# Log-sum-exp over rows: joined bulk loads, a shifted row mix, and the store's wait moved to the end of SyncE's closing waits

## Chip, cores and metric

The kernel runs on one core of one Trainium2 chip. The metric is the device time of one execution in microseconds. "Span" is what the trace of one profiled execution covers from its first to its last instruction; the measured time of the same execution is about 1.8 us longer.

## The reference

```python
def setup_inputs():
    batch, seq, dim = 32, 512, 1024
    return {"x": np.random.randn(batch, seq, dim).astype(np.float32)}

def reference(x):
    max_x = np.max(x, axis=-1, keepdims=True)
    return (max_x.squeeze(-1) + np.log(np.sum(np.exp(x - max_x), axis=-1))).astype(np.float32)
```

There are 16384 rows of 1024 floats: 67.1 MB to read and 64 KB to write. The kernel lays them out as 128 partitions with 128 rows each ("row" below is one row in every partition).

## The kernel before

It takes the exponential without subtracting the maximum, sums, takes the logarithm, and checks at the end that all sums were in a safe range. A slow path, never taken with these inputs, redoes everything with the maximum.

```python
RING = 48                      # rows of buffer in each partition
loads = [
    "R6 R5 R5", "R6 R5 R5", "R8 R8", "R8 R8", "R4 R4 R3 R3 A A", "R6 T3 T3", "R6 A A", "R4 T2",
    "R3 R3", "R3", "A A A", "R2 A", "T2", "T2", "T1", "A", "A",
]
```

Each string is one load and what is done with its rows. ScalarE always computes the exponential. For "R" VectorE reduces the rows, for "T" VectorE adds a row's two halves with an accumulator, for "A" ScalarE accumulates by itself, one instruction for each row.

```python
def load(p0, c0, size, i):
    step = {2: 4, 3: 2, 4: 2}.get(i, 1)      # loads 2, 3, 4 in interleaved pieces
    return [nc.sync.dma_start(out=ring[k::step, p0 : p0 + size, :],
                              in_=source(c0, size)[k::step]).ins for k in range(step)]
# ... cut: the loop over loads
if how == "A":
    exp = nc.scalar.activation(out=o, in_=v, func=AF.Exp, accum_out=sums)
else:
    exp = nc.scalar.activation(out=v, in_=v, func=AF.Exp)
# ... cut
if how == "R":
    added = [nc.vector.reduce_sum(out=sums, in_=v, axis=AX.X)]
elif how == "T":
    ...  # scalar_tensor_tensor(lo, lo, 1.0, hi, mult, add, accum_out=sums of the row)
# ... cut: after row 118, ScalarE's logarithm of the first 112 columns and a first check
nc.scalar.activation(out=res[:, W:NC], in_=sumexp[:, W:NC], func=AF.Ln)
nc.sync.dma_start(out=out_rows, in_=res[:, 0:W])
nc.sync.dma_start(out=out_rest, in_=res[:, W:NC])      # the last store, 8 KB
# ... cut: last check, then a branch that ScalarE and VectorE take from its result
```

All transfers are issued by SyncE. They use eight completion semaphores in turn, numbered 102, 103 and 105 to 110 in the trace. At the end SyncE waits for all eight and for the other engines. These waits stand at and in front of an instruction that the trace calls a drain (six records from 159.94 to 161.09 us, the drain at 161.16), and after it all engines meet in a closing barrier (from 161.16 us on).

## Time and profile before

| | before |
|---|---|
| time | 163.68 us, median of 3 (163.54 to 163.72) |
| span of the profile | 162.0 us |
| HBM read | 67.11 MB at 415 GB/s over the span |
| VectorE, ScalarE busy | 123.2 us, 116.2 us |
| last load complete | 158.11 us |

The page gives busy time by engine and by DMA queue; windows give the same for stretches of time; a waits line says engine, line of the kernel, what ended the wait, then total us, number, longest. The one thing that no view prints is the landing of each transfer; the trace has it as the completions on the transfer's semaphore, 384 for the 24 transfers, so 16 each, and the landing times below are the last of each 16.

### The profile page before, as it was taken

The page shows a single profiled execution, that of the slowest core. Times are in us where ns is not written, and L with a number is a line of the kernel's source. Part 1 is how long each engine was busy: PE and PEld are TensorE (multiplying, and loading weights), DVE is VectorE, ACT ScalarE, POOL GpSimd, SP SyncE. Part 2 cuts the span into 40 slices and gives each one's busy share as a digit, 9 for nine tenths or more (in the row PEclk, how much of TensorE's full clock was granted, in tenths as well). Part 3 has the DMA queues.
Part 4 walks back from the last instruction along what each step waited for, and adds up shares of the span by engine and source line. Part 5 has one row for each costly group of instructions (what it writes and reads, how often), then busy time and mean ns, then how long its engine had stood idle before and what let it go on. Part 6 is the DMA issues. An engine that isn't in the chain of part 4 may idle for free.

```text
span 162.0 us, 224 instructions
## 1 busy us (share of the span) xinstructions
PE 0.6 (0%) x8; PEld 0.3 (0%) x8; DVE 123.2 (76%) x58; ACT 116.2 (72%) x50; POOL 0.2 (0%) x4
## 2 busy tenths in 40 slices
PE   0000000000000000000000000000000000000001
PEld 0000000000000000000000000000000000000000
DVE  0000002999959997299995999999999999999982
ACT  3000069980899609994299914999999998999993
POOL 0000000000000000000000000000000000000000
DMA  7997997998899899799699698899899999999990
GB/s 275 502 518 340 437 518 340 437 518 388 388 518 421 356 518 437 340 518 486 291 518 486 291 518 388 388 449 457 388 429 435 431 395 425 431 419 415 420 359 6
DMA packets 2818, 67.19 MB, mean 415 GB/s; under 512 B 640, under 2 KB 640, under 8 KB 1024
## 3 DMA queue, kind: packets, MB, share of 16 engines
q1 hardware_dynamic: 2816, 67.18, 96.9%
q14 instruction: 2, 0.02, 0.0%
HBM read 67.11 MB, written 0.07 MB: 415 GB/s over the span
## 4 chain that ended last, share of the span: by engine, by line
DMA 52%; DVE 36%; ACT 9%; issue 1%; SPq 0%; PE 0%; DVEq 0%; ACTq 0%
DMA ring<-in_x_dram 52%; DVE sumexp L143 35%; ACT ring L133 9%; DVE ring L148 1%; SPq L88 0%; DVE bad L195 0%; PE count L199 0%; DVE clamped L105 0%; DVE bad L196 0%; DVE fine L201 0%; DVE clamped L109 0%; PE count L200 0%; DVEq L195 0%; DVEq L105 0%; ACTq L133 0%
## 5 line engine op out<-in xcount | busy, mean ns | idle before, releaser
L143 DVE TENSOR_REDUCE sumexp<-ring 128x3 f32<-128x3072 f32 (+5 forms) x21 | 113.9, 5479 | 34.1 <-ACT ring L133 34.0
L133 ACT ACTIVATE ring<-ring 128x3072 f32<-128x3072 f32 (+6 forms) x27 | 104.4, 3921 | 42.5 <-DMA ring<-in_x_dram 42.5
L131 ACT ACTIVATE ring<-ring 128x1024 f32<-128x1024 f32 x9 | 9.4, 1040 | 0.0
L148 DVE SCALAR_TENSOR_TENSOR ring<-ring 128x512 f32<-128x512 f32 x13 | 8.3, 687 | 0.7 <-ACT ring L133 0.7
L75 ACT ACT_TABLE_LOAD x1 | 1.3, 1283 | 0.8 <-PEq L262 0.8
L131 ACT ACTIVATION_READ_ACCUMULATOR ring<-ring 128x1 f32 x9 | 1.7, 186 | 0.0
L148 DVE DVE_READ_ACCUMULATOR ring<-ring 128x1 f32 x13 | 1.1, 84 | 0.0
L131 ACT ACTIVATE last_exp<-ring 128x1024 f32<-128x1024 f32 x1 | 1.0, 1028 | 0.0
L113 PE MATMUL count<-far,bad 128*1 128x1 f32 x4 | 0.4, 164 | 158.5 <-DVE clamped L109 158.5
L76 DVE MEMSET ones<- 128x1 f32 x1 | 0.1, 59 | 0.9 <-PEq L262 0.9
L105 DVE TENSOR_SCALAR clamped<-sumexp 128x118 f32<-128x118 f32 (+1 forms) x2 | 0.4, 198 | 0.2
L195 DVE TENSOR_REDUCE bad<-ring 128x1 f32<-128x64 f32 x1 | 0.2, 220 | 0.4 <-issue 0.4
L109 DVE SCALAR_TENSOR_TENSOR clamped<-clamped,sumexp 128x118 f32<-128x118 f32 (+1 forms) x2 | 0.5, 226 | 0.1
L113 PEld LDWEIGHTS count<-far,bad 128*1 128x1 f32 x4 | 0.2, 80 | 158.6 <-DVE clamped L109 158.6
L201 DVE TENSOR_SCALAR fine<-count 1x1 int32<-1x1 f32 x1 | 0.1, 147 | 0.3 <-PE count L200 0.3
L168 ACT ACTIVATE res<-sumexp 128x112 f32<-128x112 f32 x1 | 0.3, 279 | 0.0
L188 ACT ACTIVATE res<-sumexp 128x16 f32<-128x16 f32 x1 | 0.2, 215 | 0.0
L199 PE MATMUL count<-far,bad 128*1 128x1 f32 x2 | 0.2, 164 | 0.6 <-DVE bad L196 0.6
L200 PE MATMUL count<-ones,sumexp 128*1 128x1 f32 x2 | 0.2, 163 | 0.0
L131 ACT ACTIVATION_READ_ACCUMULATOR last_exp<-ring 128x1 f32 x1 | 0.2, 186 | 0.0
L196 DVE TENSOR_SCALAR bad<-bad 128x1 f32<-128x1 f32 x1 | 0.2, 154 | 0.0
L109 DVE DVE_READ_ACCUMULATOR clamped<-clamped,sumexp 128x1 f32 x2 | 0.2, 84 | 0.0
(7 smaller groups left out, 0.6 us busy)
## 6 DMA issues: line engine op xcount, KB each, us to landing
ring<-in_x_dram SPq DMA_DIRECT2D x1, 6144.0 KB, 28.8
ring<-in_x_dram SPq DMA_DIRECT2D x2, 3072.0 KB, 28.0
ring<-in_x_dram SPq DMA_DIRECT2D x3, 1536.0 KB, 29.5
ring<-in_x_dram SPq DMA_DIRECT2D x1, 4096.0 KB, 27.7
ring<-in_x_dram SPq DMA_DIRECT2D x2, 1024.0 KB, 30.2
ring<-in_x_dram SPq DMA_DIRECT2D x3, 512.0 KB, 26.1
ring<-in_x_dram SPq DMA_DIRECT2D x10, 37.6
out_dram<-res SPq DMA_DIRECT2D x1, 56.0 KB, 8.9
```

The costliest lines, as they stand in the source:

```text
L75: nc.scalar.preload_act_table_set("natural_log_exp_and_others")
L105: nc.vector.tensor_scalar(out=clamped[:, c0:c1], in0=sumexp[:, c0:c1], scalar1=LOW, scalar2=HIGH, op0=ALU.max, op1=ALU.min,)
L109: counted = nc.vector.scalar_tensor_tensor(out=clamped[:, c0:c1], in0=clamped[:, c0:c1], scalar=0.0, in1=sumexp[:, c0:c1], op0=ALU.bypass, ...
L113: nc.tensor.matmul(count, lhsT=bad[:, i : i + 1], rhs=far, start=i == 0, stop=False)
L131: exp = nc.scalar.activation(out=o, in_=v, func=AF.Exp, accum_out=sums)
L133: exp = nc.scalar.activation(out=v, in_=v, func=AF.Exp)
L143: added = [nc.vector.reduce_sum(out=sums, in_=v, axis=AX.X)]
L148: nc.vector.scalar_tensor_tensor(out=lo, in0=lo, scalar=1.0, in1=ring[:, p + r, H:d], op0=ALU.mult, op1=ALU.add, accum_out=sums[:, r : r + 1],
L168: ln = nc.scalar.activation(out=res[:, 0:W], in_=sumexp[:, 0:W], func=AF.Ln)
L188: nc.scalar.activation(out=res[:, W:NC], in_=sumexp[:, W:NC], func=AF.Ln)
L195: nc.vector.reduce_max(out=bad[:, 3:4], in_=last_row[:, 0, 0 : d // 16], axis=AX.X)
L196: nc.vector.tensor_scalar(out=bad[:, 2:3], in0=bad[:, 3:4], scalar1=LOG_LOW, scalar2=None, op0=ALU.is_lt)
```

## The change

The intent: fewer transfers and fewer waits on the way (loads 2, 3 and 4 as one transfer each), less work for VectorE in the second half at some cost to ScalarE, and nothing but the barrier left for SyncE to do once the last store has landed.

```diff
     loads = [
-        "R6 R5 R5", "R6 R5 R5", "R8 R8", "R8 R8", "R4 R4 R3 R3 A A", "R6 T3 T3", "R6 A A", "R4 T2",
-        "R3 R3", "R3", "A A A", "R2 A", "T2", "T2", "T1", "A", "A",
+        "R6 R5 R5", "R6 R5 R5", "R8 R8", "R8 R4 R4", "R4 R4 R3 R3 A A", "R6 T3 A A A", "R6 A A",
+        "R2 A A T2", "R3 R3", "R3", "A A A", "T2 A", "T2", "T2", "T1", "A", "A",
     ]
...
-        dmas = load(p, c, size, i)
+        dma = nc.sync.dma_start(out=ring[:, p : p + size, :], in_=source(c, size)).ins
...
+    def look_at_store_last(program):
+        ... # finds SyncE's drain with its list of waits
+        store = last_store.sync_info.on_update[0].id
+        waits = sorted(drain.sync_info.on_wait, key=lambda wait: wait.id != store)
+        ... # the drain gets this list: the store's wait first
+    nc.at_finalize(look_at_store_last)
...
-    nc.sync.dma_start(out=out_rest, in_=res[:, W:NC])
+    last_store = nc.sync.dma_start(out=out_rest, in_=res[:, W:NC]).ins
```

The first wait of the list stays with the drain, and the others become waits in front of it; so "first in the list" is "last in time".

More of the change, by code (lines that the diff above doesn't have):

```diff
@@ L81, in source @@
         return x_rest[:, c0 - W : c0 - W + size, :] if c0 >= W else x_rows[:, c0 : c0 + size, :]
-    def load(p0, c0, size, i):
-        step = {2: 4, 3: 2, 4: 2}.get(i, 1)
-        return [
-            nc.sync.dma_start(
-                out=ring[k::step, p0 : p0 + size, :], in_=source(c0, size)[k::step]
-            ).ins
-            for k in range(step)
-        ]
     def without_wait(ins, group, reason):
@@ L122 @@
             p = 0
-        dmas = load(p, c, size, i)
+        dma = nc.sync.dma_start(out=ring[:, p : p + size, :], in_=source(c, size)).ins
         if i == 0:
-            first_load = dmas[0]
+            first_load = dma
         for how, s in ops:
@@ L153 @@
             for add in added:
-                for dma in dmas:
-                    tc.declare_no_dep(add.ins, dma, reason="ScalarE has waited for it")
+                tc.declare_no_dep(add.ins, dma, reason="ScalarE has waited for it")
                 without_wait(add, "loads", "they came before this one")
@@ L164 @@
             last_row = v
-        for dma in dmas:
-            tc.add_to_no_dep_group("loads", dma)
+        tc.add_to_no_dep_group("loads", dma)
         if c == LATE:
@@ L184, in start_early @@
         top.insert(k, first)
+    def look_at_store_last(program):
+        block, k, drain = next(
+            (b, k, i) for b in program.main_func.blocks for k, i in enumerate(b.instructions)
+            if i.engine == mybir.EngineType.SP and isinstance(i, mybir.InstDrain)
+            and i.sync_info and len(i.sync_info.on_wait) > 2
+        )
+        store = last_store.sync_info.on_update[0].id
+        waits = sorted(drain.sync_info.on_wait, key=lambda wait: wait.id != store)
+        assert waits[0].id == store and len(waits) == len(drain.sync_info.on_wait)
+        sync = mybir.SyncInfo(on_wait=waits, on_update=list(drain.sync_info.on_update))
+        block.instructions[k] = drain.__replace__(sync_info=sync)
     nc.at_finalize(start_early)
+    nc.at_finalize(look_at_store_last)
     nc.scalar.activation(out=res[:, W:NC], in_=sumexp[:, W:NC], func=AF.Ln)
     nc.sync.dma_start(out=out_rows, in_=res[:, 0:W])
-    nc.sync.dma_start(out=out_rest, in_=res[:, W:NC])
+    last_store = nc.sync.dma_start(out=out_rest, in_=res[:, W:NC]).ins
     check(LATE, LAST, 1)
```

## The prediction

> **What bounds the kernel now.** I read the page's head and queues first, then the stages, then the waits of ScalarE, VectorE and SyncE, and last the timeline of the end, because the three parts of the change touch the transfers, the row mix and the end.
>
> ```profile
> span 162.0 us, 224 instructions
> PE 0.6 (0%) x8; PEld 0.3 (0%) x8; DVE 123.2 (76%) x58; ACT 116.2 (72%) x50; POOL 0.2 (0%) x4
> q1 hardware_dynamic: 2816, 67.18, 96.9%
> HBM read 67.11 MB, written 0.07 MB: 415 GB/s over the span
> ```
>
> The 16 DMA engines are busy for 96.9% of the span with 67.11 MB that have to be read whatever the kernel does; VectorE and ScalarE idle for a quarter of it. The stages (start:end, length, then busy time of each engine, clock, DMA share, GB/s) show where the last 3% are:
>
> ```profile
> 0.00:21.80 21.80, 0.00 (x0) 0.00 (x0) 0.09 (x2) 1.28 (x1) 0.20 (x4) 1.00 1.03 433
> 21.80:60.50 38.70, 0.00 (x0) 0.00 (x0) 31.35 (x6) 28.08 (x6) 0.00 (x0) 1.00 1.00 434
> 60.50:99.20 38.70, 0.00 (x0) 0.00 (x0) 32.86 (x5) 27.90 (x4) 0.00 (x0) 1.00 0.99 427
> 99.20:138.10 38.90, 0.00 (x0) 0.00 (x0) 38.84 (x20) 37.74 (x19) 0.00 (x0) 1.00 0.98 421
> 138.10:158.20 20.10, 0.19 (x2) 0.09 (x2) 19.23 (x22) 19.88 (x19) 0.00 (x0) 1.00 0.97 402
> 158.20:162.00 3.80, 0.43 (x6) 0.22 (x6) 0.87 (x6) 1.29 (x3) 0.00 (x0) 1.00 0.04 6
> ```
>
> The DMA share stays at 0.97 or above until 158.2 us (a packet is counted where it starts, hence 1.03). Between 99.2 and 158.2 us both compute engines are as full as the DMA, so this is where they could become the bound; the last 3.8 us belong to no transfer of input. Packet by packet, the first 64 KB packet starts at 1.02 us, the last input packet ends at 157.63 us, and the last row's landing is complete at 158.11 us; in between hardly any time has fewer than 15 packets in flight. So the time is: 158.1 us of streaming, 3.85 us of closing, and 1.7 us that the measured time (163.68 us) has over the span.
>
> The waits say who follows whom:
>
> ```profile
> ACT ring L133 <- DMA ring<-in_x_dram: 42.5, 7, 19.7
> DVE sumexp L143 <- ACT ring L133: 34.0, 4, 26.2
> SPq L88 <- DVE sumexp L143: 98.4, 10, 22.7
> ```
>
> ScalarE waits for loads, VectorE for ScalarE, and SyncE for slots that VectorE frees. The last looks like a bound but is none: each load is issued long before the queue is empty. The load issued at 44.53 us follows one that lands at 60.46; 63.86 follows 79.81; 84.94 follows 99.16; 95.67 follows 113.69; 104.26 follows 123.41; the last at 138.05 follows 156.83. The smallest lead is 14.2 us.
>
> The end, from the timeline:
>
> ```profile
> 156.24 0.69 DVE L148 SCALAR_TENSOR_TENSOR ring<-ring 128x512 f32<-128x512 f32 x1 [0.69 <-ACT ring L133]
> 157.06 1.04 ACT L131 ACTIVATE ring<-ring 128x1024 f32<-128x1024 f32 x1
> 158.13 1.03 ACT L131 ACTIVATE last_exp<-ring 128x1024 f32<-128x1024 f32 x1
> 159.31 0.21 ACT L188 ACTIVATE res<-sumexp 128x16 f32<-128x16 f32 x1
> 159.55 0.34 SPq L190 DMA_DIRECT2D out_dram<-res  x1
> 159.81 0.15 DVE L201 TENSOR_SCALAR fine<-count 1x1 int32<-1x1 f32 x1 [0.33 <-PE count L200]
> ```
>
> The last row's exponential starts 0.02 us after its landing, so neither engine is late there; the store's issue follows it at 159.55 us and lands at 161.08.
>
> [...] 433 to 434 GB/s in the first stages, before packets get small. [...] the unsplit second load lands 19.33 us after the first (41.11 after 21.78), the split ones 19.35 us after their predecessors (60.46, 79.81, 99.16). [...] 1040 ns for 1024 elements, 7020 for 8192, and rows of "A" start 1.04 us apart, so the accumulator read of 186 ns is hidden in the overlap. [...] SyncE's record on the store's semaphore begins at 161.094, 0.014 us after the landing.
>
> **The change part by part.**
>
> *Bulk loads as one transfer.* Loads 2, 3 and 4, of 8.39 MB each, were 4 + 2 + 2 transfers; they become 3. Bytes, packet size (64 KB, one per partition) and number of data packets stay. Removed are five issues of SyncE (0.33 to 0.62 us each, all of them behind a full queue, so worth nothing) and five completion markers on each DMA engine: 3 x (19.35 - 19.33) = 0.06 us of streaming. ScalarE also stops waiting for two to four semaphores before these loads: it starts 0.11 us after landing (60.57 against 60.46) where an unsplit load takes 0.02 (41.13 against 41.11). That is off the path, as ScalarE waits over 5 us for each of these loads.
>
> *Row mix.* From the groups by form, VectorE: R rows (reduce) cost about 1.09 us each (9.87 us for nine, in the timeline from 141.61 us), T rows 0.615 us (start to start), A rows nothing. Three T become A: -1.84; two R become A: -2.2; two R become T: -0.95; one R8 becomes two R4: about 2 x 4.41 - 8.68 = +0.14. Some 4.9 us less for VectorE. ScalarE: three A for one T3 is 3 x 1.04 - (2.75 - 0.09) = +0.46; R2 and two A for R4 is (1.90 - 0.09) + 2.08 - (3.61 - 0.09) = +0.37; R2 to T2 is the same exponential; R8 to two R4 is +0.1 and lies in front of a wait of 5.4 us. So +0.83 us where it matters, between 99.24 and 138.06 us. There ScalarE waits 1.11 us in one place, for the load that lands at 138.03. The 0.83 us fit in, and 0.28 us is left. From 138.06 on the order of ScalarE's work is unchanged. VectorE's gain goes into waiting for ScalarE: at 156.24 us it is already idle for 0.69 us before the last T rows. Neither engine's part moves the last landing or the start of the last exponential. Worth 0.00 us.
>
> *The last wait.* SyncE ends with a row of two-semaphore waits, some 60 ns each when satisfied, then two drains into the closing barrier. In this kernel's program the first wait in an instruction's list stays with the instruction, and the others go in front of it; the store is in the last pair in front of the drain. Put first in the list, it is waited for in the drain itself, and what stands between (161.094 to 161.161) is no longer behind the landing: 0.067 us earlier on SyncE, whose barrier entry moves from 161.223 to about 161.156. But the barrier waits for all engines, and ScalarE enters it at 161.257 (a drain of 97 ns that begins at 161.160, 0.37 us after its last branch); GpSimd goes on at 161.289. So ScalarE is the last by 0.03 us, and SyncE's 0.067 us give almost nothing unless ScalarE's comes earlier. I count 0.02.
>
> Sum: -0.06 + 0.00 - 0.02 = -0.08 us: 163.68 becomes 163.60 us.
>
> **The rivals.**
>
> *ScalarE becomes the bound.* For it: 19.88 of 20.10 us busy from 138.1 to 158.2, and it gets ten more instructions. If my 0.83 us were 1.3, it would start the load of 138.03 late by 0.2 us; but it catches up, for later it waits 0.22 us at 154.29 and the rows until then have slack of some tenths. If it doesn't catch up, the lateness goes one to one to the end: 163.8 to 164.1 us. Against: the activations are all measured, and the sum has little room.
>
> *The last landing moves earlier because slots come free earlier.* For it: SyncE's 98.4 us of waiting for VectorE. Against: the lead of 14 us or more; the queue is never empty. If I misread and it does, at most the streaming's loss against 433.6 GB/s (67.11 MB take 154.8 us, against 156.6 from the first packet to the last) could come back, 1.8 us: 161.9 us. But that loss is the slow first packets (3.1 instead of 2.42 us, some 0.7 us) and the small packets of the tail, and both stay.
>
> *Small stalls move.* VectorE's reduction before the finiteness check begins 0.42 us after the instruction before it with no wait that the trace shows, ScalarE's drain is 0.37 us late likewise, and near 142 us all packets of 12 KB are slow for a while (0.25 us in one load's landing). Instruction counts shift by -2 on VectorE and +10 on ScalarE, so such stalls may move: 0.1 to 0.4 us either way on the closing chain. If ScalarE's drain came earlier, the full 0.067 us of the wait would count.
>
> *The split loads did something good* that their joining loses, such as keeping the queue's start quick. Against: loads 0 and 1 are unsplit, and stream at 434 GB/s.
>
> **Range and chances.** The kernel's own runs lie within 0.18 us. Estimated effects are 0.1 us or less, the stalls up to 0.4: 163.25 to 163.95 us should hold it 8 times in 10. Two per cent is 3.3 us; to gain it the kernel would have to finish before its bytes are in, and to lose it ScalarE would need over four times the added 0.83 us. Faster 0.01, within 2% 0.98, slower 0.01.
>
> **What would show it.** In the changed profile: 2736 packets on q1 (five transfers fewer, 16 completions each) and 67.18 MB; VectorE near 118.2 us busy in 56 instructions, ScalarE near 118.1 in 60; VectorE's wait for ScalarE about 5 us longer in total; ScalarE starting the three bulk loads 0.02 instead of 0.08 to 0.11 us after landing; no empty queue; the last exponential near 158.1; the closing chain still about 3.85 us. I am wrong if ScalarE begins the last row visibly after its landing, if the DMA share falls below 0.97 before the last row, or if the span after the last landing shrinks by much more than 0.07 us.

The 0.09 us between two activations in a row can be read in the trace: three of 2.749 us each took 8.07 us together from 138.06 us, 0.09 us of overlap at each of the two seams.

## The result

| | before | changed |
|---|---|---|
| time, median (range), 6 runs each | 163.67 us (163.54 to 163.74) | 163.64 us (163.55 to 163.91) |
| ratio, 95% interval | | 1.0002 (0.9989 to 1.0015) |
| span of the profile | 161.96 us | 161.76 us |
| last load complete | 158.11 us | 157.95 us |
| last store, issue to landing | 1.53 us | 1.59 us |
| landing to SyncE's drain | 0.08 us | 0.02 us |

A ratio is the mean time of one kernel's runs over that of the other's runs of the same rounds, so not quite the ratio of the medians. The time has not changed.

The page's head of the changed kernel:

```profile
span 161.8 us, 221 instructions
PE 0.8 (0%) x8; PEld 0.3 (0%) x8; DVE 118.5 (73%) x56; ACT 117.2 (72%) x60; POOL 0.2 (0%) x4
q1 hardware_dynamic: 2736, 67.18, 97.0%
```

There are 80 packets fewer for the same bytes. VectorE lost 4.7 us of work and ScalarE gained 1.0. The windows of the second half:

```profile
99.20:138.10 38.90, 0.00 (x0) 0.00 (x0) 36.55 (x15) 38.59 (x28) 0.00 (x0) 1.00 0.98 422
138.10:158.20 20.10, 0.19 (x2) 0.09 (x2) 16.90 (x26) 20.07 (x19) 0.00 (x0) 1.00 0.96 399
158.20:162.00 3.80, 0.57 (x6) 0.26 (x6) 0.69 (x6) 1.14 (x3) 0.00 (x0) 1.00 0.04 6
```

VectorE, 38.84 of 38.90 us busy before in the first of these, is at 36.55; ScalarE fills the second stretch all but completely. The DMA share and the GB/s are those of before to 0.01 and 3 GB/s. ScalarE's start on the load that lands at 138 us, before and changed:

```profile
138.06 8.07 ACT L133 ACTIVATE ring<-ring 128x3072 f32<-128x3072 f32 x3 [1.11 <-DMA ring<-in_x_dram]
138.08 8.07 ACT L122 ACTIVATE ring<-ring 128x3072 f32<-128x3072 f32 x3 [0.28 <-DMA ring<-in_x_dram]
```

Its longer work has taken 0.83 us of the wait there, and it still starts on time. Where VectorE's time went, in the waits:

```profile
ACT ring L122 <- DMA ring<-in_x_dram: 41.3, 6, 19.7
DVE sumexp L132 <- ACT ring L122: 37.2, 6, 26.2
DVE ring L137 <- ACT ring L122: 2.1, 2, 1.5
```

VectorE waits 39.3 us for ScalarE instead of 34.7. The end, from the timeline:

```profile
157.98 1.03 ACT L120 ACTIVATE last_exp<-ring 128x1024 f32<-128x1024 f32 x1
159.16 0.22 ACT L190 ACTIVATE res<-sumexp 128x16 f32<-128x16 f32 x1
159.40 0.34 SPq L192 DMA_DIRECT2D out_dram<-res  x1
159.40 0.14 DVE L203 TENSOR_SCALAR fine<-count 1x1 int32<-1x1 f32 x1 [0.59 <-PE count L202]
```

The last exponential still starts 0.02 us after the last landing, and everything else of the end hangs on it as before. The check's result comes 0.41 us earlier, but nothing waits for it alone.

### The profile page after: what moved, and what is told of

Read it like the earlier page. It is cut to its first block, busy times and chain, and to the rows that moved or that the text cites. A ratio compares the mean times of both kernels' runs of the same rounds, so it can differ in the third digit from the quotient of the medians.

```text
span 161.8 us, 221 instructions
## 1 busy us (share of the span) xinstructions
PE 0.8 (0%) x8; PEld 0.3 (0%) x8; DVE 118.5 (73%) x56; ACT 117.2 (72%) x60; POOL 0.2 (0%) x4
## 4 chain that ended last, share of the span: by engine, by line
DMA 53%; DVE 35%; ACT 10%; issue 1%; PE 0%
DMA ring<-in_x_dram 53%; DVE sumexp L132 35%; ACT ring L122 9%; ACT ring L120 1%; ACT last_exp L120 0%; PE count L202 0%; DVE fine L203 0%
## 5 line engine op out<-in xcount | busy, mean ns | idle before, releaser
L132 DVE TENSOR_REDUCE sumexp<-ring 128x3 f32<-128x3072 f32 (+5 forms) x21 | 109.5, 5276 | 37.2 <-ACT ring L122 37.2
L122 ACT ACTIVATE ring<-ring 128x3072 f32<-128x3072 f32 (+6 forms) x27 | 100.3, 3763 | 41.4 <-DMA ring<-in_x_dram 41.3
L120 ACT ACTIVATE ring<-ring 128x1024 f32<-128x1024 f32 x14 | 14.6, 1040 | 0.0
L137 DVE SCALAR_TENSOR_TENSOR ring<-ring 128x512 f32<-128x512 f32 x12 | 7.7, 687 | 2.1 <-ACT ring L122 2.1
L120 ACT ACTIVATION_READ_ACCUMULATOR ring<-ring 128x1 f32 x14 | 2.6, 187 | 0.0
```

The lines of the kernel that those rows point to most:

```text
L137: nc.vector.scalar_tensor_tensor(out=lo, in0=lo, scalar=1.0, in1=ring[:, p + r, H:d], op0=ALU.mult, op1=ALU.add, accum_out=sums[:, r : r + 1],
```

## The experiments

Twelve kernels ran, each profiled once and timed in up to five rounds beside the kernel before. The table has what the traces show at the end; the texts follow.

| run | time us, median | ratio (95%) | last load complete | store, issue to landing | landing to SyncE's drain |
|---|---|---|---|---|---|
| before again | 163.75 | 0.9998 (0.9986, 1.0010) | 158.24 | 1.58 | 0.09 |
| wait only | 163.67 | 0.9998 (0.9986, 1.0010) | 158.15 | 1.54 | 0.02 |
| loads only | 163.96 | 1.0014 (1.0003, 1.0026) | 158.07 | 1.53 | 0.39 |
| row mix only | 164.11 | 1.0023 (1.0010, 1.0036) | 158.22 | 1.81 | 0.09 |
| changed, store's wait first | 164.06 | 1.0024 (1.0009, 1.0038) | 157.94 | 1.64 | 0.39 |
| changed, eight pieces | 270.05 | 1.6495 (1.6472, 1.6518) | 264.08 | 1.79 | 0.02 |
| changed, light engines | 163.55 | 0.9986 (0.9971, 1.0000) | 158.43 | 1.43 | 0.02 |
| changed, more A | 165.06 | 1.0079 (1.0065, 1.0094) | 158.43 | 1.42 | 0.02 |
| before, two rows to VectorE | 165.10 | 1.0087 (1.0073, 1.0101) | 157.91 | 1.93 | 0.09 |
| changed, two rows to VectorE | 163.60 | 0.9994 (0.9980, 1.0007) | 157.95 | 1.64 | 0.02 |
| changed, both padded | 164.32 | 1.0034 (1.0020, 1.0048) | 158.88 | 1.42 | 0.02 |
| changed, VectorE padded | 164.07 | 1.0020 (1.0006, 1.0034) | 158.72 | 1.43 | 0.02 |

### Before again

No edit.

> The kernel before, unchanged, against itself. It measures what two identical programs differ by, and whether three oddities of the first profile belong to the program or to that one execution: VectorE's 0.42 us without a wait before its last reduction, ScalarE's closing drain that starts 0.37 us after its last branch, and the slow packets near 142 us. If they belong to the program, the new profile has all three at the same places. If they belong to the execution, some are gone or elsewhere and the span is shorter by up to 0.3 us, with no change of the kernel. Timed: ratio 1.000, with an interval of about 0.001.

The ratio is 0.9998. Two of the three oddities belong to the program: VectorE's last reduction again comes late with no wait, and ScalarE's closing drain again begins 0.36 us after its last branch. The slow packets near 142 us are not there (that load lands 3.69 us after the one before it, not 3.91), so they do not belong to the program. The first load landed at 22.11 us instead of 21.78, though: a single trace's landing times are good to some 0.3 us, and only the steps between landings, where nothing disturbs them, are good to 0.02.

### Each part alone

Wait only: the kernel before with the function and the `last_store` of the diff.

> The kernel before with the store's wait moved into SyncE's drain and nothing else. Prediction's theory: SyncE's first drain starts right at the store's landing instead of 0.08 us after it, the waits between are done before; of the 0.067 us between 0.00 and 0.07 reach the end, by whether ScalarE's drain is late. Timed 163.60 to 163.68, not to be told from zero. Rival, that the wait was a real cost: 0.3 us or more off the time.

Loads only:

```diff
-        step = {2: 4, 3: 2, 4: 2}.get(i, 1)
+        step = 1
```

> The kernel before with each of loads 2, 3 and 4 as one transfer and nothing else. The prediction said that five markers fewer give 0.06 us of streaming: bulk loads landing 19.33 us apart. The profile of the changed kernel contradicts it (19.35 us apart, as split); then here too 19.35, and the last landing moves only by what varies from execution to execution (0.2 us). ScalarE starts the bulk loads 0.02 us after landing in both cases. Rival, that splitting helped the queue: 0.3 us or more slower. Timed: within 0.1 us of before.

Row mix only: the two lines of `loads` of the diff.

> The kernel before with the changed row mix and nothing else. Theory: VectorE 118.4 us busy, ScalarE 117.2, VectorE idle 4 us more before its instructions, ScalarE's wait for the load that lands at 138.0 us shrinks from 1.11 to about 0.28 us, the last exponential still starts within 0.05 us of the last landing; time within 0.1 us of before. Rival, that ScalarE's longer work reaches the end: 0.2 us or more slower. Rival, that slots freed earlier speed up the stream: 0.3 us or more faster and a last landing before 157.7 us.

The wait alone did what was expected: the drain starts 0.02 us after the landing, and the time is the same. In that trace ScalarE enters the barrier at 161.29 and SyncE at 161.22 us, so the gain is swallowed there.

The loads alone are slower by 0.2 to 0.3 us, which the theory didn't have, and the rival only for another reason. It isn't the stream: the bulk loads land 19.35 us apart, as in pieces. It is SyncE's end. SyncE's wait for the store after its last issue, in the kernel before, in the loads alone and in the changed kernel:

```profile
SPq L273 <- DMA out_dram<-res: 0.2, 1, 0.2
```

```profile
SPq L273 <- DMA out_dram<-res: 1.2, 1, 1.2
```

```profile
SPq L275 <- DMA out_dram<-res: 0.4, 1, 0.4
```

A longer wait here means that SyncE came to the store's semaphore earlier and had its other waits still to do when the store landed. The trace says why. With 24 transfers the store uses semaphore 110, which is in the last of the closing waits. With 19 it uses 105, which is in the first. So in the loads alone SyncE waits for 105 until 161.07 us and then goes through five more waits, 0.06 us each, and reaches its drain at 161.44, 0.39 us after the landing. The transfer count had moved the store's wait to the worst place, and the third part of the change moves it away again. Parts one and three belong together.

The row mix alone is 0.4 us slower, and the engines are not the reason. ScalarE's last exponential starts 0.03 us after the last landing, and its wait for the load that lands at 138 us did shrink as expected. Two other steps are longer in its trace: one load lands 3.84 us after the one before where 3.69 is usual, and the store takes 1.81 us to land instead of 1.53 and 1.58 in the two traces of the kernel before. This is taken up with the padded kernels below.

### The store's wait in the first place

```diff
+        waits = waits[1:7] + waits[:1] + waits[7:]     # after the sort: the first wait in time
```

> The changed kernel with the store's wait put in the first of SyncE's closing waits, so that all the others come after the landing. It enlarges the disputed cost: five more waits of about 0.06 us behind the landing. Theory: SyncE enters the closing barrier 0.30 to 0.36 us later after the store's landing than in the changed kernel, and as SyncE is last there, the time is 0.3 us longer: 163.95 us. Rival, that the other engines hold the barrier and SyncE's order is of no account: 163.64 us.

It was 164.06 us; the drain begins 0.39 us after the landing against 0.02, and all other landings are those of the changed kernel to 0.03 us.

```profile
SPq L276 <- DMA out_dram<-res: 1.3, 1, 1.3
```

The theory holds, and the order of SyncE's waits costs up to 0.4 us in this kernel. The trace shows SyncE's waits in the same order here as in the loads alone, so this run also stands for the changed kernel without its third part.

### Eight pieces for each bulk load

```diff
-        dma = nc.sync.dma_start(out=ring[:, p : p + size, :], in_=source(c, size)).ins
+        step = 8 if i < 5 else 1
+        dmas = [nc.sync.dma_start(out=ring[k::step, p : p + size, :],
+                                  in_=source(c, size)[k::step]).ins for k in range(step)]
```

> The changed kernel with each of the five bulk loads as eight transfers of every eighth partition: 35 transfers more. It enlarges the prediction's 0.012 us for each transfer saved. If that were right, 35 x 0.012 = 0.42 us more: 164.06 us, bulk loads landing 19.43 us apart. If markers cost nothing while the engines are saturated, as the two profiles together suggest: 19.35 us apart and 163.64 us. Rival, that more issues delay the stream's start: the first load lands later than 21.8 us.

It took 270 us, and failed as a test of the markers, because something far larger came in. A window in the bulk loads of the changed kernel, the same window here, and one after the bulk loads, where loads are whole again:

```profile
22.00:60.00 38.00, 0.00 (x0) 0.00 (x0) 30.83 (x6) 27.90 (x6) 0.00 (x0) 1.00 1.00 435
22.00:60.00 38.00, 0.00 (x0) 0.00 (x0) 11.06 (x2) 14.04 (x3) 0.00 (x0) 1.00 0.96 198
222.00:262.00 40.00, 0.19 (x2) 0.09 (x2) 33.48 (x28) 39.46 (x34) 0.00 (x0) 1.00 1.00 424
```

The DMA engines are busy for 0.96 of the window but move less than half as much: most 64 KB packets take 5.10 us instead of 2.42. Every eighth partition in a piece gave 198 GB/s against the 435 of whole loads. The pieces land 5.10 to 5.12 us apart (the very last after 5.01), but 4.86 to 4.91 us apart where piece 4 follows piece 3 or the next load's piece 0 follows piece 7. The five loads lost 106 us together. Load 2 of the kernel before, in four pieces of every fourth partition, lost nothing: its pieces land 4.82 to 4.85 us apart, 19.35 us together. Why every eighth partition is slow and every fourth is not, no run here shows. As for the markers, the loads-only run answers: 19.35 us for a bulk load in one, two or four pieces.

### Light engines

```diff
-            v = ring[:, p : p + s, :]
+            n = d if c == LAST else d // 8       # wrong results on purpose
+            v = ring[:, p : p + s, 0:n]          # T rows likewise on halves of n
```

> The changed kernel with ScalarE and VectorE working on the first 128 of 1024 columns of every row but the last: wrong results on purpose. All bytes are still loaded, slots come free far earlier, and the closing is unchanged. Theory (the stream of bytes sets the time and no slot delays it): last landing within 0.2 us of 158.0, time within 0.2 us of 163.64. Rival (slots come free too late somewhere): up to 1.8 us faster, last landing down to 156.2 us.

With nearly no work for ScalarE and VectorE and slots free much earlier, the time is 163.55 us. The last load completes at 158.43, which is later than expected and 0.48 us later than in the changed kernel, not earlier (this profile fell on the slowest of the four runs, 163.87 us). ScalarE's total wait:

```profile
ACT ring L124 <- DMA ring<-in_x_dram: 130.7, 14, 19.7
```

So the stream sets the time, no slot delays it, and by the interval of this run no shift of rows between engines can gain more than some 0.5 us.

### More rows on ScalarE

```diff
-        "R6 T3 A A A", ... "R2 A A T2"
+        "A A A A A A A A A A A A", ... "A A A A A A"
```

> The changed kernel with all rows of the sixth and eighth load summed by ScalarE: by 1.04 us for a row alone against 0.854 us a row plus 0.1 us for each group, 2.0 us more for ScalarE before the load that lands at 138.0 us. Theory: 0.28 us of it is taken by the wait there and about 0.1 us near 154 us, the rest reaches the end: the last exponential starts about 1.6 us after the last landing, 165.2 us. Rival (ScalarE catches up, or its work does not set the end): 163.6 us.

It was 165.06 us. The last exponential starts 1.56 us later than in the changed kernel:

```profile
159.54 1.00 ACT L120 ACTIVATE last_exp<-ring 128x1024 f32<-128x1024 f32 x1
```

Against its own last landing (158.43, itself late in this trace) it is 1.1 us behind. The cost of a row by start-to-start times was right, and most of what ScalarE doesn't have time for goes to the end: it starts the load of 138 us 1.77 us later than in the changed kernel (139.85 against 138.08), and catches up only 0.2 us of that. The row mix uses its room up to about 0.3 us.

### Two more rows on VectorE, before and after

```diff
-        "R4 R4 R3 R3 A A"
+        "R4 R4 R3 R3 R2"
```

> The kernel before with two rows of the fifth load summed by VectorE instead of ScalarE: 2.2 us more for VectorE, 0.3 us less for ScalarE. It asks how much slack VectorE had. Theory: VectorE runs without a pause from 87 to 151 us, the logarithm of the first 112 columns waits for its sums and had 1.0 us to spare, so ScalarE stalls there by about 1.2 us and most of it reaches the end: 164.5 to 164.9 us. Rival (VectorE is off the path with room): 163.7 us.

> The changed kernel with the same two rows moved to VectorE. Theory: the row mix gave VectorE 4 us of idle time, 2.35 us of it right behind these rows, so the 2.2 us vanish there: 163.6 us, within 0.1 us of the changed kernel, where the same edit costs the kernel before about 1 us. Rival (the row mix gave no room that counts): 164.5 us.

The kernel before loses 1.4 us, somewhat more than expected, the changed one nothing. In the kernel before with this edit, ScalarE's first logarithm waits for VectorE's sums:

```profile
150.33 0.30 ACT L168 ACTIVATE res<-sumexp 128x112 f32<-128x112 f32 x1 [1.06 <-DVE sumexp L143]
```

The last exponential starts at 158.96, 1.05 us after its landing; the rest is the store, which takes 1.93 us instead of 1.53. The same stretch of VectorE in the changed kernel, without and with the edit:

```profile
130.08 6.55 DVE L132 TENSOR_REDUCE sumexp<-ring 128x6 f32<-128x6144 f32 x1 [2.35 <-ACT ring L122]
```

```profile
130.09 6.55 DVE L132 TENSOR_REDUCE sumexp<-ring 128x6 f32<-128x6144 f32 x1 [0.16 <-ACT ring L122]
```

The 2.2 us vanish in an idle time of 2.35. That is what the row mix bought: not time, but room on VectorE, which in the kernel before had about 1.1 us left before that logarithm needs its sums (2.2 us added, 1.06 us waited).

### Padding the instruction streams

In every trace in which the store took over 1.5 us, 15 of its 16 completions came by 1.45 us and one came late. Beside the data, the DMA engines also carry instruction fetches of 8 KB on a queue of their own (q14: two packets of 8192 bytes in the span of the kernel before, at 159.73 and 161.79 us). One fetch ended 0.55 to 1.02 us after the store's issue in all of them, and broadly the later the fetch the later the completion (0.55 and 1.54 in the wait alone, 0.82 and 1.81 in the row mix alone, 1.02 and 1.93 in the kernel before with two rows). The late completion follows the end of its fetch by 0.87 to 1.02 us in all ten. The two traces without such a fetch had 1.42 and 1.43: more A has no fetch near its store, and in light engines the last one ended 0.16 us after the issue. The test:

```diff
     nc.vector.memset(far, 100 * HIGH)
+    for _ in range(24):
+        nc.vector.memset(pad_v, 0.0)
+    for _ in range(24):                                  # in the first of the two runs only
+        nc.scalar.activation(out=pad_s, in_=ones, func=AF.Exp)
```

> The changed kernel with 24 tiny instructions more on VectorE and on ScalarE, all in the first 20 us in which both wait for the first load. In eleven profiles the last of the store's 16 completions is late only where an 8 KB instruction fetch ends at most about 1 us before it (1.53 to 1.93 us after the issue; 1.42 and 1.43 in the two without). Theory [...]: the longer programs are fetched earlier, in the middle of the stream; no fetch from 158 us to the store's landing, which comes 1.43 us after its issue; 0.16 us off the closing: 163.45 to 163.5 us. Rival (coincidence): the fetches move and the store still takes 1.55 to 1.65 us, 163.64 us.

> The changed kernel with the 24 tiny instructions on VectorE alone. It tells which engine's fetch holds up the store. If the last fetch before the landing (0.20 us after the store's issue in the changed kernel) is VectorE's: it is gone from there and the store lands 1.43 us after its issue, as in the run with both. If it is ScalarE's: the fetch stays and the store takes 1.55 to 1.65 us, 163.64 us. A fetch from another engine: both runs keep it.

The store landed after 1.42 and 1.43 us, as the theory said; the rival falls. (With VectorE alone padded a fetch still runs at 159.81 us, but it ends 0.14 us after the issue, as early as the one in light engines.) But the time rose by about 0.6 and 0.4 us, which no theory had. With VectorE padded, a fetch came at 154.57 us, among the last loads. The one-row load in flight then lands 2.01 us after the one before instead of 1.29: 15 of its 16 completions are in at 155.44, the sixteenth comes at 156.18, and one completion stays 0.7 us behind in both loads that follow (the trace doesn't name the engine of a completion). ScalarE then waits where it didn't in the changed kernel:

```profile
157.49 1.06 ACT L123 ACTIVATE ring<-ring 128x1024 f32<-128x1024 f32 x1 [0.23 <-DMA ring<-in_x_dram]
158.75 1.03 ACT L123 ACTIVATE last_exp<-ring 128x1024 f32<-128x1024 f32 x1
```

With both padded there is a fetch at 117.83 us too, and the load then in flight takes 10.08 us instead of 9.72. In the run with more A a fetch at 127.36 goes with a step of 7.69 instead of 7.31, and in the row mix alone one at 142.29 goes with the 3.84 instead of 3.69. So in these four traces a fetch in the stream goes with a landing 0.15 to 0.7 us late, and with VectorE padded the two landings after it stay 0.7 us late.

A fetch is not the only thing that lengthens a step: the first trace of the kernel before has one of 3.91 us and the light engines one of 4.00, both without a fetch in flight. The completions tell the two apart. There all 16 come late alike, by 0.1 us and by 0.26 us in the median. In the steps with a fetch 15 keep the usual distance from the load before and one is late, by an estimate from the sorted completions 0.7 to 1.0 us. Not all of that shows in the step from landing to landing: in the row mix alone 0.15 us of 0.75.

In the changed kernel the two fetches come at 159.07 and 159.60 us, after the stream, where only the store pays, 0.15 us or so.

Why a completion comes late after a fetch that itself ended 0.87 to 1.02 us before it, the runs don't show. Whose stream a fetch belongs to is only partly settled: padding VectorE moved the fetch that met the store (159.60 us in the changed kernel, 154.57 then), so that one follows VectorE's stream; the other one, near 159 us (159.07, and 159.81 with VectorE padded), went only when ScalarE was padded too.

No version here beat the two kernels clear of noise.

## Why the prediction was right, point by point

- **The stream sets the time.** Right, and the light engines show it directly, to within 0.5 us.
- **Joined loads, 0.06 us.** Wrong in its size: bulk loads land 19.35 us apart in one piece or in four. The 19.33 us from which it was worked out is the step after the first load, and that step is 19.31 to 19.34 in the split kernels and 19.32 to 19.35 in the unsplit ones, so it says nothing of splitting. The step also missed what the joining does elsewhere: it moves the store's semaphore from the last to the first of SyncE's closing waits, which costs 0.3 us by itself. So the rival that the split loads did something good was right, but not for the reason it gave. That pieces cost nothing held for every second and fourth partition (19.35 us a load), not for every eighth (64 KB packets of 5.10 us instead of 2.42).
- **Row mix, 0.00 us.** Right. ScalarE's wait at 138 us shrank from 1.11 to 0.28 us, as worked out; VectorE waits 4.6 us longer for ScalarE; nothing moved at the end. ScalarE's busy time, put at 118.1 us, is 117.2: the sum counted each overlap of neighbouring instructions twice, while the 0.83 us by start times, used for the argument, was right.
- **The wait, 0.02 us.** The number is within noise and the 0.067 us on SyncE were right (0.08 to 0.02 us from landing to drain), but the working compared with the wrong kernel. Given the joined loads, the order is worth 0.3 to 0.4 us: loads alone against all three parts, and the reversed order. It gains nothing over the kernel before because there the store's wait happened to be last already.
- **Small stalls move by 0.1 to 0.4 us.** Right in size, and for ScalarE's drain and VectorE's reduction also in kind: both are gone in the changed kernel. What the rival didn't name is the largest disturbance of the kind, the instruction fetches, which cost up to 0.7 us. The row mix alone, with 0.4 us, most likely shows this: in each of its two long steps one completion is late beside a fetch. That was seen in one trace, and in the padded runs, where fetches were moved; in the row mix alone itself they weren't moved.
- **Its signs and readings.** ScalarE starts the three bulk loads 0.02 us after landing, as forecast. One sign of being wrong did come: the DMA share from 138.1 to 158.2 us is 0.96. It means nothing here, as the last load completes 0.16 us earlier in that same window. And a record of SyncE is not always free of waiting: that of the store's wait begins with the landing, as read (0.017 us after it, not 0.014), but that of another wait for two semaphores, at 160.12 us, lasts 0.65 us, where the others take 0.03.
- **The sum, 163.60 us.** Measured 163.64. That it came so close is partly luck: a forecast of -0.08 us can't be told from zero with an interval of about 0.2 us either way, and there are terms that cancel, 0.3 us lost by the joining and gained back by the wait, and fetches that fall differently in each version. The wait, the loads and the row mix alone measure 0.0, +0.3 and +0.4 us, and together 0.0: with effects of this size they don't add.

## What to carry to other kernels

Here the stream of bytes kept the DMA engines busy for 0.96 or more of each stretch up to 158 us, and moving work between the compute engines bought room (2.35 us of idle time on VectorE) and not time (163.64 against 163.67 us). Test for that by making the engines nearly idle, as in the light engines (163.55 us). Look at where the last store's completion stands among the closing waits whenever the number of transfers changes: here its place was worth 0.39 against 0.02 us from landing to drain. Before trusting a difference of 0.3%, look at where the instruction fetches fall; here one went with a landing up to 0.7 us late. And measure a split of a transfer by partitions before relying on it: pieces of every second or fourth partition cost nothing here (19.35 us a load), pieces of every eighth more than halved the rate (198 against 435 GB/s).
